# Hybrid attention block on one core: other durations and priorities in attention's list scheduler

## Chip, cores and metric

One core of a Trainium2 chip runs the whole kernel. The metric is the device time of one execution in microseconds (us). Three executions of the kernel before took 3311.18, 3316.16 and 3320.15 us; their median, 3316.16 us, is the time that the change is held against.

## What is computed

One transformer layer over 2048 tokens and 16 meta tokens, width 1024, in fp32: RMSNorm and one input projection, two groups of attention heads side by side, an output projection with a residual, then RMSNorm and a SwiGLU feed-forward part with a residual. Cut to the two attention groups:

```python
# group A: 8 query heads, 2 key heads, head width 64
p = jax.nn.softmax(sc, axis=-1).astype(va.dtype)
o = jnp.einsum('bkgql,blkd->bqkgd', p, va)
# group B: 4 heads; queries and keys in two halves j, values 128 wide
sc = jnp.einsum('bqhjd,blhjd->bhjql', q, kb).astype(jnp.float32) * scale
p = jax.nn.softmax(sc, axis=-1)
w = (p[:, :, 0] - lam * p[:, :, 1]).astype(vb.dtype)
o = jnp.einsum('bhql,blhe->bqhe', w, vb)
```

## The kernel before, in words

The kernel has three parts that follow each other: the input projection, attention, and output projection with the feed-forward part. Attention stands in an order that the kernel works out itself before anything runs; the other two parts are untouched.

Fp32 accuracy is had from fp16: a value is split into a high half (a cast) and a low half (value minus high half), and products are summed from the halves.

**Group B** has 64 *steps*, one for 128 queries of one head. Line numbers are those of the kernel before; in the changed kernel they are one higher from line 53 on. For each of its two score halves a step runs: score matmuls into a PSUM buffer `sy` (`score`, L482, PE); the *drain* of that buffer into SBUF with a running minimum (`minimum`, L489, DVE, 128x1024 a time, four a step); a bias (`peak`, L522, DVE); the exponential with its sum (`expo`, L517, ACT). Then two factors (L528, L532, DVE), the *difference* of the two halves (`diff`, L536, DVE, in two pieces), the cast to fp16 (`fp16_hi`, L112 with output `p`, ACT or DVE), the low half of that (`fp16_lo`, L549, five pieces, mostly POOL), a transposing DMA (`turn`, L585, on SP's queue) and 50 products with V (`pv`, L594, PE).

**Group A** has 32 *groups* of 128 queries and four heads. First a *reach*: plain scores into `sy` (`reach`, L498, PE) and their minimum over the keys (`lowest`, L502, DVE, eight of 128x1024 a group), a *merge* of these (L979, DVE), a flip of the merged column into a row (L985, PE) and the row itself (L992, DVE or ACT). Then nine *chunks* of turned scores: matmuls into `sy` (L512, L513, PE), exponential (`expo_a`, L555, ACT), high half (`hi_a`, L112 with output `hl`, ACT or DVE), *low half* (`lo_a`, L561, POOL or DVE), products with V (`pv_a`, L570, PE).

So three buffers `sy` are shared by everything that PE scores, and are freed by DVE (drain, reach, row) or ACT (chunks). One group and two steps make a *round*: from one merge L979 to the next. There are 32 merges.

The **list scheduler** (the loop at the end of attention) holds a list of tasks per engine. A task has a time from which it may start, an estimated cost, the buffers that it needs and an age. At each turn the engine that can start something earliest takes, of the tasks that can start then, the one with the lowest age, emits its instructions and frees itself after the estimated cost. `wait` and `later` add, for one engine of those that may take a task, a delay and an age. Tasks marked with `port` (low halves, differences, casts on DVE) are planned so that DVE and POOL never run one at the same time. The estimates only shape the order: on the chip each engine runs its instructions in that order, and semaphores do the rest.

```python
at = [(max([z["ready"] + z["wait"].get(n, 0.0), idle[n], port[0] if n in z["port"] else 0.0] + [when(k) for k in z["need"]]), z["age"] + z["later"].get(n, 0.0), i)
      for i, z in enumerate(todo[n])]
```

## Time and profile before

| | before |
|---|---|
| median of 3 runs (lowest, highest) | 3316.16 us (3311.18, 3320.15) |
| the profiled execution | 3310.24 us |
| its span, first to last instruction | 3308.4 us |
| mean granted TensorE clock | 0.99 |
| busy share of the span: PE, DVE, ACT, POOL | 95%, 62%, 50%, 50% |

The busy shares are averages over three parts with different limits. The page's chain that ended last gives PE 72%, DVE 11%, ACT 6%, time in which an engine waited for nothing that the profile shows 5%, DMA 4%. The largest lines of that chain, L1379 with 27% and L1340 with 14%, belong to the feed-forward part; those of attention (L594, L570, L482, L489, L555, L502, L536) have 2 to 4% each.

A row of the timeline gives start, duration, engine, line, operation, output<-input and count; a count over 1 means that neighbours of the same kind were merged. In brackets stands the idle time of the engine before it and what ended it.

### The profile page before, as it was taken

The numbers are of one execution on the slowest core, as the hardware profiler recorded it, in microseconds if no ns is written. First come the engines' busy times: TensorE is split into PE (matmuls) and PEld (weight loads), VectorE is DVE, ScalarE is ACT, GpSimd is POOL, SyncE is SP. The second block draws the span as 40 slices with busy tenths as digits, with TensorE's granted clock in tenths as the row PEclk, the third lists the DMA queues.
The fourth block names the chain that finished last, engine by engine and source line by source line (L and its number), as shares of the span: only waits on it lengthen the run. The fifth ranks groups of instructions, "written<-read, shape, count | busy, mean of one in ns | idle before, by whom it ended". The sixth has DMA issues, their size and how long they took to land.

```text
span 3308.4 us, 57942 instructions
## 1 busy us (share of the span) xinstructions
PE 3145.7 (95%) x23043; PEld 2069.5 (63%) x23043; DVE 2056.2 (62%) x3656; ACT 1639.2 (50%) x1991; POOL 1639.3 (50%) x1597
## 2 busy tenths in 40 slices
PE   8999988989988898888889999999999999999999
PEld 7999975655555565555568755555555555555555
DVE  7555568888888889888865334444444544444445
ACT  6333328888887888888866222222222322222220
POOL 6888866767676677676721133232232323232231
PEclk9999999999999999999999999999999999999999
DMA  5322233343243334433467511111111511111111
GB/s 168 72 68 68 67 85 74 78 109 88 73 111 81 84 86 100 88 83 74 107 236 259 165 58 55 42 58 42 54 52 45 174 50 51 45 58 39 57 45 51
DMA packets 503359, 281.35 MB, mean 85 GB/s; under 512 B 330704, under 2 KB 478624, under 8 KB 502576
## 3 DMA queue, kind: packets, MB, share of 16 engines
q1 hardware_dynamic: 501376, 275.14, 30.6%
q8 instruction: 181, 2.97, 0.4%
q10 hardware_dynamic: 1712, 2.51, 0.3%
q14 instruction: 90, 0.74, 0.1%
HBM read 168.44 MB, written 39.93 MB: 63 GB/s over the span
## 4 chain that ended last, share of the span: by engine, by line
PE 72%; DVE 11%; ACT 6%; issue 5%; DMA 4%; POOL 1%; SPq 0%; DVEq 0%; ACTq 0%; POOLq 0%
PE pg L1379 27%; PE psd L1340 14%; PE pl L269 10%; PE sy L482 4%; PE ob L594 4%; PE oa L570 3%; DVE e L489 3%; ACT et L555 2%; DVE mna L502 2%; PE ps L1285 2%; PE sy L498 2%; PE sy L512 2%; PE sy L513 2%; DVE e L536 2%; DMA wq<-in_w_up_dram 1%
## 5 line engine op out<-in xcount | busy, mean ns | idle before, releaser
L1342 DVE TENSOR_TENSOR y<-psd,y 128x512 f32<-128x512 f32 x704 | 484.8, 691 | 551.0 <-PE psd L1340 549.8
L561 POOL TENSOR_TENSOR hl<-et,hl 128x1024 f16<-128x1024 f32 (+1 forms) x247 | 520.9, 2128 | 303.8 <-ACT hl L112 168.7
L1379 PE MATMUL pg<-h2h,e 128*128 128x512 f16 x2112 | 660.0, 380 | 1.6 <-POOL e L116 1.6
L1379 PEld LDWEIGHTS <-e 128*128 128x128 f16 x3168 | 283.2, 98 | 390.3 <-issue 84.9
L1379 PE MATMUL pg<-h2l,e 128*128 128x512 f16 x1056 | 400.7, 380 | 0.0
L489 DVE CUSTOM_DVE_ANT_0 e<-sy,zero,mn 128x1024 f32<-128x1024 f32 x256 | 325.5, 1277 | 43.0 <-PE sy L482 37.8
L116 POOL TENSOR_TENSOR e<-qa,e 128x1024 f16<-128x1024 f32 (+1 forms) x44 | 100.0, 2273 | 498.8 <-issue 381.8
L555 ACT ACTIVATE et<-sy,lnpa,ndq 128x1024 f32<-128x1024 f32 (+1 forms) x288 | 322.1, 1145 | 39.6 <-PE sy L513 16.9
L549 POOL TENSOR_TENSOR p<-e,p 128x516 f16<-128x516 f32 (+2 forms) x320 | 311.4, 1006 | 50.7 <-ACT p L112 49.6
L1381 ACT ACTIVATE th<-pg,unh 128x512 f32<-128x512 f32 x88 | 60.5, 688 | 532.3 <-PE pg L1379 525.4
L1340 PE MATMUL psd<-kt,kt 128*128 128x512 f32 x1056 | 323.0, 434 | 0.0
L502 DVE TENSOR_REDUCE mna<-sy 128x1 f32<-128x1024 f32 x256 | 311.3, 1217 | 16.1 <-PE sy L498 15.5
L1340 PE MATMUL psd<-e,e 128*128 128x512 f32 x1056 | 320.5, 432 | 0.7 <-DVE y L1342 0.7
L517 ACT ACTIVATE e<-e,bs,ndq 128x2064 f32<-128x2064 f32 x128 | 269.2, 2103 | 92.2 <-DVE bs L522 92.2
L482 PE MATMUL sy<-kt,qb 128*128 128x512 f16 (+1 forms) x1280 | 284.3, 342 | 30.5 <-DVE mn L489 9.9
L570 PEld LDWEIGHTS <-hl 128*128 128x128 f16 (+1 forms) x6528 | 241.6, 97 | 91.3 <-issue 20.5
L570 PE MATMUL oa<-va,hl 128*128 128x65 f16 (+3 forms) x6528 | 261.8, 193 | 21.0 <-DVE hl L561 7.9
L112 ACT CAST hl<-et 128x1024 f16<-128x1024 f32 (+1 forms) x288 | 275.8, 991 | 6.8 <-PE oa L570 5.3
L116 POOL TENSOR_TENSOR kt<-qb,kt 128x1024 fp32r<-128x1024 f32 x22 | 52.7, 2397 | 442.8 <-issue 384.2
L594 PEld LDWEIGHTS <-pt 128*128 128x128 f16 (+2 forms) x3200 | 202.2, 98 | 72.9 <-issue 7.8
L1340 PEld LDWEIGHTS psd<-e,e 128*128 128x128 f32 x1056 | 198.8, 189 | 59.0 <-DVE y L1342 1.2
L1340 PEld LDWEIGHTS psd<-kt,kt 128*128 128x128 f32 x1056 | 199.0, 189 | 58.5
(229 smaller groups left out, 5775.4 us busy)
## 6 DMA issues: line engine op xcount, KB each, us to landing
wq<-in_w_gate_dram SPq DMA_DIRECT2D x16, 704.0 KB, 4.9
wq<-in_w_up_dram SPq DMA_DIRECT2D x16, 704.0 KB, 5.4
qa<-in_w_gate_dram SPq DMA_DIRECT2D x22, 512.0 KB, 3.9
qa<-in_w_down_dram SPq DMA_DIRECT2D x22, 512.0 KB, 3.7
qa<-in_w_up_dram SPq DMA_DIRECT2D x22, 512.0 KB, 3.8
qb<-in_w_up_dram SPq DMA_DIRECT2D x22, 512.0 KB, 3.7
qb<-in_w_down_dram SPq DMA_DIRECT2D x22, 512.0 KB, 3.6
qb<-in_w_gate_dram SPq DMA_DIRECT2D x22, 512.0 KB, 3.8
```

The lines of the kernel that those rows point to most:

```text
L269: T.matmul(ps[:rows, c0:UW], hb[:, a, k, :rows], w_at(w, ui, k)[:, c0:], start=(k == 0 and a == 0 and w == 0), stop=(k == KD - 1 and a == 1))
L482: T.matmul(y[:, (c - c0) // 512 if g_ else j, :n], qt[:, j, a, qi * P:(qi + 1) * P], kt[:, c:c + n], start=(a == 0), stop=(a == 1))
L489: V.tensor_tensor_reduce(e[:, c0:c1], src[:, :c1 - c0], zero.broadcast_to([P, c1 - c0]), 1.0, mn[:, g_ - 1:g_] if g_ else big, ALU.add, AL ...
L502: V.tensor_reduce(g["mn"][:, h, g_:g_ + 1], y.rearrange("p b n -> p (b n)"), axis=AX.X, op=ALU.min)
L549: eng.tensor_tensor(out=p[:, at + c0:at + c1], in0=st["e"][0][:, c0:c1], in1=p[:, c0:c1], op=ALU.subtract)
L555: A.activation(of(et, k), of(y, k), AF.Exp, bias=lnpa if k else lnpa[:NM], scale=ndq[:, 0:1] if k else ndq[:NM, 0:1])
L561: eng.tensor_tensor(out=of(z[:, 1], k), in0=of(et, k), in1=of(z[:, 0], k), op=ALU.subtract)
L570: T.matmul(o[:, h, :wn], z[:rows, a, i, h * P:(h + 1) * P], vt[:rows, c, vh, :wn], start=(first and h == 0 and n == 0), stop=(last and n = ...
L594: T.matmul(o, pt[:rows, blk, :], vt[:rows, c, vh, :], start=(c == 0 and n == 0), stop=(c == NC - 1 and n == 1))
L1340: T.matmul(ps, a[:, i * P:(i + 1) * P], w[:, 0, ns], start=(ii == 0), stop=(ii == 2))
L1342: V.tensor_tensor(out=yt[:, ns], in0=ps, in1=yt[:, ns], op=ALU.add)
L1379: T.matmul(ps, a[:, k], b_[:, k], start=(k == 0 and ii == 0), stop=(k == KD - 1 and ii == 2))
```

## The change

Only constants of the scheduler change, and six estimates.

- Estimated durations: the drain L489 1.22 to 1.36 us (`CM`); the reach keeps 1.22 under a name of its own (`CR`); the bias 0.07 to 0.12; the exponential of group B 2.0 to 2.29, of a chunk 1.08 to 1.19 (its small first chunk 0.6 to 0.75).
- Ages (lower goes first): turned scores `OPT` -2 to -1.5; drain and reach on DVE `OM` -2 to -1; group B's and the reach's scores on PE `OP` -2 to -1; bias, merge, flip and row `OB` -2 to 0; low half `OL` 3 to 0; products with V `OV` -10 to -10.5, which makes them later by 0.5.
- Which engine: DVE may take a chunk's low half without the 2 us delay that it had (`LWA` 2 to 0), at an age higher by 1 (`LLA` 0 to 1); DVE's high half of a chunk gets 6 instead of 3 (`HLA`).
- `HCUT` 2 to 1: a cast to fp16 that DVE took would be one piece, not two.

```diff
-HCUT = 2
+HCUT = 1
...
-CM = 1.22
+CM = 1.36
+CR = 1.22
...
-OPT = -2.0
-LWA, LLA, HWA, HLA = 2.0, 0.0, 50.0, 3.0
-OS, OX, OM, OD, OH, OP, OV, OE = -2.0, -1.0, -2.0, -2.0, 3.0, -2.0, -10.0, 2.0
+OPT = -1.5
+LWA, LLA, HWA, HLA = 0.0, 1.0, 50.0, 6.0
+OS, OX, OM, OD, OH, OP, OV, OE = -2.0, -1.0, -1.0, -2.0, 3.0, -1.0, -10.5, 2.0
...
-OB, OC, OL = -2.0, 0., 3.0
+OB, OC, OL = -2.0, 0., 0.0
...
-                            task(("act",), st["n"] + OX, end + X_, 2.0, x)
-                        task(("dve",), st["n"] + OB, end + 0.14, 0.07, bias)
+                            task(("act",), st["n"] + OX, end + X_, 2.29, x)
+                        task(("dve",), st["n"] + OB, end + 0.14, 0.12, bias)
...
-                task(("dve",), g["n"] - GS + h * GS / 4 + OM, end + 0.2, CM if g_ else 0.25, m)
+                task(("dve",), g["n"] - GS + h * GS / 4 + OM, end + 0.2, CR if g_ else 0.25, m)
...
-                task(("act",), age + OX, end + 0.2, 1.08 if k else 0.6, x, ("et",))
+                task(("act",), age + OX, end + 0.2, 1.19 if k else 0.75, x, ("et",))
```

What this makes of the order is seen at three places, all on DVE. In the rows `hl<-et` is a low half, `e<-e,rho,e` a difference, `e,mn<-sy` a drain, `mna<-sy` a reach, `qa<-sy` the row; numbers tell buffers apart.

The first place is the start of a late round, from the merge of the 27th group on. Before:

```order
L979 TENSOR_REDUCE mqa_19866<-mna_19476 128x4
L522 TENSOR_SCALAR bs_19883<-mn_19649,dq_102,lnpk_100 128x1
L561 TENSOR_TENSOR hl3_6614<-et3_6610,hl3_6614 128x1024
L992 TENSOR_SCALAR qa0_6581<-sy2_6619 1x512
L489 ISA e0_6585,mn_19942<-sy0_6617,zero_65,big_67 128x16
L489 ISA mn_19942 128x1
L489 ISA e2_6587,mn_19943<-sy0_6617,zero_65,big_67 128x16
L489 ISA mn_19943 128x1
L528 RECIPROCAL rc_19965<-sums_19647 128x2
L532 SCALAR_TENSOR_TENSOR rho_19967<-rc_19965,neglam_94,sums_19647 128x1
L536 SCALAR_TENSOR_TENSOR e4_6589<-e1_6586,rho_19967,e4_6589 128x1032 x2
L504 TENSOR_REDUCE mna_19988<-sy0_6617 128x4
```

and now:

```order
L980 TENSOR_REDUCE mqa_19851<-mna_19491 128x4
L607 TENSOR_SCALAR mix_19695<-ob0_6720,rc_19486 128x128
L523 TENSOR_SCALAR bs_19858<-mn_19663,dq_102,lnpk_100 128x1
L993 TENSOR_SCALAR qa0_6581<-sy0_6617 1x512
L537 SCALAR_TENSOR_TENSOR e4_6589<-e5_6590,rho_19744,e4_6589 128x1032 x2
L562 TENSOR_TENSOR hl5_6616<-et1_6608,hl5_6616 128x1024
L529 RECIPROCAL rc_19958<-sums_19661 128x2
L533 SCALAR_TENSOR_TENSOR rho_19972<-rc_19958,neglam_94,sums_19661 128x1
L490 ISA e2_6587,mn_19952<-sy2_6619,zero_65,big_67 128x16
L490 ISA mn_19952 128x1
L490 ISA e3_6588,mn_19953<-sy2_6619,zero_65,big_67 128x16
L490 ISA mn_19953 128x1
```

A whole difference that stood in the round before is now behind the row, and behind the rows shown the second difference follows; in this round DVE has three differences, in its neighbours one.

The second place is the middle of the same round, where the second step of the round begins. Before:

```order
L502 TENSOR_REDUCE mna_19988<-sy0_6617 128x1
L489 ISA e5_6590,mn_20188<-sy0_6617,zero_65,big_67 128x16
L489 ISA mn_20188 128x1
L489 ISA e3_6588,mn_20189<-sy0_6617,zero_65,big_67 128x16
L489 ISA mn_20189 128x1
L528 RECIPROCAL rc_20221<-sums_19941 128x2
L532 SCALAR_TENSOR_TENSOR rho_20226<-rc_20221,neglam_94,sums_19941 128x1
```

and now:

```order
L562 TENSOR_TENSOR hl2_6613<-et0_6607,hl2_6613 128x1024
L562 TENSOR_TENSOR hl3_6614<-et1_6608,hl3_6614 128x1024
L529 RECIPROCAL rc_20190<-sums_19951 128x2
L490 ISA e5_6590,mn_20127<-sy2_6619,zero_65,big_67 128x16
L490 ISA mn_20127 128x1
L490 ISA e0_6585,mn_20128<-sy2_6619,zero_65,big_67 128x16
L490 ISA mn_20128 128x1
L533 SCALAR_TENSOR_TENSOR rho_20203<-rc_20190,neglam_94,sums_19951 128x1
L537 SCALAR_TENSOR_TENSOR e2_6587<-e3_6588,rho_20203,e2_6587 128x1032 x2
```

Two low halves have come to DVE here, ahead of the factors.

The third place is the end of attention, around the last difference. Before:

```order
L561 TENSOR_TENSOR hl1_6612<-et3_6610,hl1_6612 128x1024
L561 TENSOR_TENSOR hl2_6613<-et0_6607,hl2_6613 128x1024
L606 TENSOR_SCALAR mix_22709<-ob0_6720,rc_22520 128x128
L528 RECIPROCAL rc_22938<-sums_22674 128x2
L532 SCALAR_TENSOR_TENSOR rho_22941<-rc_22938,neglam_94,sums_22674 128x1
L536 SCALAR_TENSOR_TENSOR e4_6589<-e1_6586,rho_22941,e4_6589 128x1032 x2
```

and now:

```order
L537 SCALAR_TENSOR_TENSOR e1_6586<-e2_6587,rho_22937,e1_6586 128x1032 x2
L562 TENSOR_TENSOR hl2_6613<-et0_6607,hl2_6613 128x1024
L562 TENSOR_TENSOR hl3_6614<-et1_6608,hl3_6614 128x1024
L550 TENSOR_TENSOR p16_1_6604<-e1_6586,p16_1_6604 128x516 x3
L550 TENSOR_TENSOR p16_1_6604<-e1_6586,p16_1_6604 128x500
L550 TENSOR_TENSOR p16_1_6604<-e1_6586,p16_1_6604 128x16
L562 TENSOR_TENSOR hl4_6615<-et2_6609,hl4_6615 128x1024
L562 TENSOR_TENSOR hl5_6616<-et3_6610,hl5_6616 128x1024
```

The low halves of the last step's `p` and of the last chunks, POOL's before, stand on DVE.

Counted over the program, no instruction is added or dropped but for where they run: DVE takes 70 of the 256 full low halves of chunks instead of 41, POOL 186 instead of 215; one small low half, the five pieces of one step's `p` and three small evacuations (L606 for L604) come to DVE as well. All 64 casts to fp16 are ACT's in both, so `HCUT` cuts nothing.

## Rows read from the trace of the kernel before

**Rows 1.** The page: span, and busy time of each engine.
```profile
span 3308.4 us, 57942 instructions
PE 3145.7 (95%) x23043; PEld 2069.5 (63%) x23043; DVE 2056.2 (62%) x3656; ACT 1639.2 (50%) x1991; POOL 1639.3 (50%) x1597
```

**Rows 2.** Timeline of DVE, the merge L979: first, last and nine between.
```profile
493.40 0.17 DVE L979 TENSOR_REDUCE mqa<-mna 128x4 f32<-128x12 f32 x1
...
695.55 0.16 DVE L979 TENSOR_REDUCE mqa<-mna 128x4 f32<-128x12 f32 x1
736.91 0.16 DVE L979 TENSOR_REDUCE mqa<-mna 128x4 f32<-128x12 f32 x1
...
842.39 0.16 DVE L979 TENSOR_REDUCE mqa<-mna 128x4 f32<-128x12 f32 x1
...
914.18 0.16 DVE L979 TENSOR_REDUCE mqa<-mna 128x4 f32<-128x12 f32 x1
...
987.84 0.15 DVE L979 TENSOR_REDUCE mqa<-mna 128x4 f32<-128x12 f32 x1
1034.68 0.16 DVE L979 TENSOR_REDUCE mqa<-mna 128x4 f32<-128x12 f32 x1
...
1282.15 0.16 DVE L979 TENSOR_REDUCE mqa<-mna 128x4 f32<-128x12 f32 x1
1323.74 0.16 DVE L979 TENSOR_REDUCE mqa<-mna 128x4 f32<-128x12 f32 x1
...
1470.53 0.16 DVE L979 TENSOR_REDUCE mqa<-mna 128x4 f32<-128x12 f32 x1
...
1619.55 0.15 DVE L979 TENSOR_REDUCE mqa<-mna 128x4 f32<-128x12 f32 x1
```

**Rows 3.** Windows, the shortest full round: stretch, length, busy of PE, PEld, DVE, ACT, POOL.
```profile
1249.09:1282.15 33.06, 31.75 (x402) 20.39 (x400) 30.86 (x56) 29.56 (x29) 21.52 (x17) 1.00 0.43 106
```

**Rows 4.** Timeline of DVE in the round from the merge at 1396.05.
```profile
1396.05 0.15 DVE L979 TENSOR_REDUCE mqa<-mna 128x4 f32<-128x12 f32 x1
...
1396.35 1.22 DVE L561 TENSOR_TENSOR hl<-et,hl 128x1024 f16<-128x1024 f32 x1
1397.48 0.67 DVE L992 TENSOR_SCALAR qa<-sy 1x512 f16<-1x512 f32 x1
...
1399.70 2.50 DVE L536 SCALAR_TENSOR_TENSOR e<-e,rho,e 128x1032 f32<-128x1032 f32 x2
1403.40 0.23 DVE L504 TENSOR_REDUCE mna<-sy 128x4 f32<-128x64 f32 x1 [1.20 <-PE sy L498]
...
1412.65 3.30 DVE L561 TENSOR_TENSOR hl<-et,hl 128x1024 f16<-128x1024 f32 x1
...
1421.08 4.37 DVE L536 SCALAR_TENSOR_TENSOR e<-e,rho,e 128x1032 f32<-128x1032 f32 x2
...
1426.51 1.27 DVE L489 CUSTOM_DVE_ANT_0 e<-sy,zero,mn 128x1024 f32<-128x1024 f32 x1
...
1427.71 1.21 DVE L502 TENSOR_REDUCE mna<-sy 128x1 f32<-128x1024 f32 x1
1428.85 1.27 DVE L489 CUSTOM_DVE_ANT_0 e<-sy,zero,mn 128x1024 f32<-128x1024 f32 x1
```

**Rows 5.** Timeline of POOL, the same round.
```profile
1409.53 8.41 POOL L561 TENSOR_TENSOR hl<-et,hl 128x1024 f16<-128x1024 f32 x4
```

**Rows 6.** Groups by line and form, 490 to 1660 us: busy, mean ns, idle before.
```profile
L561 POOL TENSOR_TENSOR hl<-et,hl 128x1024 f16<-128x1024 f32 x214 | 479.8, 2255 | 289.7 <-ACT hl L112 156.5 <-issue 116.8 <-DMA qa<-mix_scr 8.7
...
L561 DVE TENSOR_TENSOR hl<-et,hl 128x1024 f16<-128x1024 f32 x41 | 68.4, 1673 | 0.5 <-issue 0.5
```

**Rows 7.** Timeline of DVE, then of POOL, at the end of attention.
```profile
1638.30 7.85 DVE L561 TENSOR_TENSOR hl<-et,hl 128x1024 f16<-128x1024 f32 x1
...
1663.89 2.15 POOL L549 TENSOR_TENSOR p<-e,p 128x516 f16<-128x516 f32 x1
...
1667.12 4.92 POOL L549 TENSOR_TENSOR p<-e,p 128x516 f16<-128x516 f32 x4
```

## The prediction

> **What bounds the kernel now.** I read the page first: PE is busy 95% of the span and DVE 62% [rows 1]. That is an average; the change reorders only attention, so I looked there, with windows and with a clock made of the merge L979, one per round. The 32 merges run from 493.40 to 1619.55 us [rows 2]: 31 rounds in 1126.15 us, 36.33 us each. Three are long because a head's keys and values are exchanged in them: 41.36, 46.84 and 41.59 us, from 695.55, 987.84 and 1282.15 [rows 2], 129.79 together. The other 28 take 996.36, a mean of 35.58 us. They differ: the best has 33.06 us [rows 3], the two from 1396.05 on have 74.48 together [rows 2, 4], 37.24 each.
>
> The best round shows the floor: PE is busy 31.75, DVE 30.86, ACT 29.56 of 33.06 us [rows 3]. Three engines are nearly full, none can be relieved much, and a longer round is one in which they wait for each other. The late round shows how. DVE stands 1.20 us at L504 because PE could not score [rows 4]: all three `sy` buffers were held by turned scores that ACT had not drained. And DVE's low half takes 3.30 us instead of 1.22, the two pieces of a difference 4.37 instead of 2.50 [rows 4]: POOL was in the middle of four low halves of 2.1 us each [rows 5], and these operations do not run beside POOL's. The planner believes that it keeps the two apart; with wrong durations it doesn't. So 2.08 and 1.87 us are lost in one round.
>
> **The change, part by part.** *Work on each engine.* 29 full low halves go from POOL to DVE. The next row starts 1.13 us after one on DVE [rows 4]; on POOL one takes 2.10 [rows 5]. DVE gains 29 x 1.13 = 33 us, about one a round; POOL loses 61. The time in which DVE and POOL exclude each other falls by 29 x (2.10 - 1.13) = 28 us over attention. The moved small pieces are a few us. `HCUT` costs nothing and gains nothing, since no cast to fp16 is on DVE.
>
> *The order.* From about the sixth round on the new order repeats every two rounds, a light one with one difference and two low halves on DVE and a heavy one with three differences and three low halves. I price DVE's work in such a pair by the distance from one start to the next: 16 drains at 1.20 and 16 reaches at 1.14 (1426.51, 1427.71, 1428.85) [rows 4], 19.2 + 18.2; eight pieces of differences at 1.21 (2.50 for two that overlap by 0.08), 9.7; five low halves at 1.13, 5.7. For the small ones (row 0.67 [rows 4], biases, factors, evacuations, small drains) I take 4.1 us a round, an estimate: of the 30.86 us of the best round [rows 3], which has two low halves, the large ones are 9.6 + 9.1 + 4.8 + 2.3, which leaves 5.0, and I take off 0.9 for the ends of records that lie in waits. Together 61.0 us a pair.
>
> Then the waits. I walked one pair of the new order forward on paper, PE, DVE, ACT and POOL side by side, with these durations and three `sy` buffers. In the light round about 2.2 us of waiting are left: 0.5 for the second exponential before the factors, 0.6 at the first drain, 0.9 at the low half ahead of the second step, behind a POOL low half, and some tenths. In the heavy round 3.8: 0.8 around the row, which now has no low half ahead of it to fill the time of the flip; 1.0 in a difference that POOL's `p` pieces enter; 0.5 at the two low halves; 1.3 at reaches and drains late in the round. The stall at L504 is gone: differences and low halves, 7 us of work, fill the time in which ACT drains turned scores. That makes 67.0. A walk on paper misses collisions, so I add one more like that of the difference, 1.87 [rows 4]: **68.9 us a pair**, 34.45 a round. Ends for the pair: 66.1, twice the best round [rows 3], and 74.5, the late pair; I take the value near the first, since the walk accounts for each wait there.
>
> Of the 28 ordinary rounds 22 have the new pattern; the first five and one with a V conversion in it I leave at their mean, and the three exchanges too, whose waits for DMAs the change doesn't touch. Gain: 11 x (2 x 35.58 - 68.9) = 25 us.
>
> *The end of attention.* Before, DVE's low half at 1638.30 takes 7.85 us [rows 7], 6.6 more than one alone, because POOL runs a low half and five `p` pieces meanwhile; drains and chunks behind it wait. And the low half of the last `p` on POOL lasts from 1663.89 to 1672.04 [rows 7], 8.15 us, with everything after it waiting. Now DVE does that. No row has these pieces on DVE: half a piece of a difference, 0.6 us each, bounds it below, 2.6 in all; a POOL-like 4.9 above. Two low halves stand before it, 2.3. I take 4 us gained of 8.15 (ends 1 and 5.5), and half of the 6.6 us, 3.3, as another low half will meet POOL: **7 us**, ends 0 and 12.
>
> *What gives back.* DVE is 61 of 68.9 us full; what is late next is the row after the flip, and POOL's `p`: in the heavy round two steps' `p` run one after the other, and their transposes reach PE with some 1.5 us to spare in the walk.
>
> *Sum.* 3310.24 us, the profiled execution, - 25 - 7 = 3278. That execution lies 0.9 us under the lowest of the three timed runs and 5.9 under their median; I add 2 and predict **3280 us**, 1.1% under the median.
>
> **A rule against the change.** A low half that meets POOL on DVE takes 1.67 us in the mean, on POOL 2.26 [rows 6]. The Trainium skill (Perfetto Trace Analysis, Optimizing Scalar/DVE Operations) says that VectorE and GpSimd share an SBUF port, so that moving work between them may not help. By this rule the sum would keep DVE's 33 us and lose the 25. The rows give a mixed picture: collisions are there, yet the same work occupies both for 1.13 us on the one engine and 2.10 on the other, so the move shortens the shared time. It is the second rival below.
>
> **The durations.** The new 1.36 for a drain is its record, 1.27, and the 0.08 of the readout behind it; but the next instruction starts after 1.20 [rows 4]. So the plan believes DVE slower than it is, by 256 x 0.16 = 41 us over attention, and the old 1.22 was nearer as a distance. That a longer estimate orders better is no matter of course; the walk, not the estimate, carries my forecast. The Trainium skill (same page and section) says that a recorded latency covers time that overlaps the next instruction, as these rows do; by it the new constant would be wrong for throughput.
>
> **Rivals.** 0.3% of 3316, 10 us, is about what a measurement of this kernel can tell from no change.
> 1. *Forecast:* pairs of 67 to 70.5 us, 3260 to 3302. Chance 0.58.
> 2. *Nothing gained:* DVE's added 33 us lie on the path and the waits only move. For it: in the pair from 842.39 to 914.18, in which DVE has four low halves, 71.79 us pass [rows 2] although POOL hardly disturbs it. With 71.8 a pair: 11 x 0.64 = +7, - 4 at the end: 3313, with the 2 us 3315. Chance 0.15, of which 0.03 is faster by over 0.3%.
> 3. *Slower: POOL enters between the pieces.* In the heavy round three differences and three low halves must each find POOL idle. Where POOL's low half is ready between two of them, it takes 2.1 us and DVE waits 1.87 [rows 4]. In my walk the margin is under 1 us at three of these places. Three more such waits make 68.9 + 5.6 = 74.5, as the late pairs have: 11 x 3.34 = +37, and no gain at the end: 3347, with the 2 us 3349. Two more (72.6) are where it becomes slower than before. Against it: POOL has 61 us less work, and stands idle behind ACT's casts 156.5 us in all [rows 6]. Chance 0.15.
> 4. *More gained:* pairs at the floor of 66.1, the end at 12 us: 11 x 5.06 + 12 = 68, 3242, with the 2 us 3244. Chance 0.12.
>
> That the change doesn't do what it says can be excluded: the order shows it.
>
> **Numbers.** Faster by over 0.3%: 0.58 + 0.12 + 0.03 = 0.73; within: 0.12; slower: 0.15. The range goes from 3246, close to the floor, to 3330, which leaves out most of rival 3; about 0.08 is outside below and 0.12 above. The forecast's own range is 3260 to 3302.
>
> **What would show it.** The distance of merges in the late rounds: two in turn, near 31 and 38 us, together 67 to 70.5; by rival 2 near 72, by rival 3 near 74. No stall of 1 us at L505 in the heavy round. Differences with 2.50 us for two pieces; where 4.4 shows up in more than one place of a pair, rival 3 is at work. POOL's busy time in attention lower by 60 us, DVE's higher by about 30 less what collisions shrink. The last `p` on DVE in under 5 us, attention's end earlier by the sum. Wrong would be my pair if DVE waits for PE at transposed `p` (L595), which never held PE up before.

## The result and the profile after

The changed kernel takes **3264.04 us** (median of 4 runs, 3262.35 to 3266.65) against 3313.67 us of the kernel before in the same comparison (4 runs, 3310.13 to 3320.15): a ratio of 0.985, 95% interval 0.983 to 0.9867, so 49.6 us or 1.5% faster. The forecast was 3280 us, 36 us under the median of 3316.16 us that it was worked out against and 34 under this one. The profiled execution of the changed kernel took 3266.65 us with a span of 3264.9 us, 43.5 us under the span before [rows 1]; the working below is against the spans.

Line numbers are one higher than before, since a constant was added. First the page of the changed kernel.

```profile
span 3264.9 us, 57936 instructions
...
PE 3130.3 (96%) x23043; PEld 2065.4 (63%) x23043; DVE 2085.0 (64%) x3694; ACT 1651.0 (51%) x1988; POOL 1574.2 (48%) x1562
```

POOL has 65 us less to do, DVE 29 us more [rows 1]. That is the moved work, and it does not tell why 43 us are gone: POOL is busy half of the span in both, and DVE is now busier.

The groups by line and form in attention tell more, 490 to 1620 us of the changed kernel (busy, mean ns; then the idle time of the engine before them, and what ended it).

```profile
L562 POOL TENSOR_TENSOR hl<-et,hl 128x1024 f16<-128x1024 f32 x186 | 410.8, 2228 | 175.0 <-ACT hl L113 102.6 <-issue 47.3 <-PE sy L986 14.4
...
L518 ACT ACTIVATE e<-e,bs,ndq 128x2064 f32<-128x2064 f32 x128 | 269.4, 2105 | 15.7 <-DVE bs L523 14.2
...
L499 PE MATMUL sy<-kt,qa 128*128 128x512 f16 x496 | 150.3, 385 | 13.3 <-DVE mn L490 7.1 <-DVE mna L503 4.1 <-DVE mna L505 1.8
...
L562 DVE TENSOR_TENSOR hl<-et,hl 128x1024 f16<-128x1024 f32 x70 | 101.7, 1468 | 0.4 <-ACT hl L113 0.3
...
L505 DVE TENSOR_REDUCE mna<-sy 128x4 f32<-128x64 f32 x31 | 6.7, 218 | 0.1
```

The same view of the kernel before, 490 to 1660 us, for three of these lines:

```profile
L517 ACT ACTIVATE e<-e,bs,ndq 128x2064 f32<-128x2064 f32 x128 | 269.2, 2103 | 92.2 <-DVE bs L522 92.2
...
L498 PE MATMUL sy<-kt,qa 128*128 128x512 f16 x496 | 150.2, 385 | 41.8 <-DVE mna L502 33.1 <-DVE mn L489 4.6 <-ACT et L555 3.1
...
L504 DVE TENSOR_REDUCE mna<-sy 128x4 f32<-128x64 f32 x31 | 7.0, 225 | 32.6 <-PE sy L498 32.6
```

Read the last column. The work per instruction is the same, but the waits have shrunk: ACT waited 92.2 us ahead of group B's exponentials for the bias on DVE, now 15.7 in all and 14.2 for the bias; PE 41.8 us ahead of the reach's matmuls, now 13.3; DVE 32.6 us for the first scores of a round, now 0.1. That last one is the stall of 1.20 us of [rows 4], which came 26 times in the kernel before.

The steady rounds are an exact clock. Windows of the changed kernel for a light and a heavy round that follow one another (columns as in [rows 3], then TensorE's granted clock, DMA share and GB/s), and for comparison the late pair of the kernel before:

```profile
1442.57:1472.83 30.26, 29.64 (x363) 19.00 (x360) 28.31 (x51) 28.76 (x29) 19.48 (x14) 1.00 0.47 97
1472.83:1509.87 37.04, 33.89 (x451) 21.80 (x449) 35.09 (x58) 32.95 (x31) 27.17 (x21) 1.00 0.33 80
```

```profile
1396.05:1470.53 74.48, 64.82 (x810) 41.36 (x807) 65.53 (x105) 60.85 (x60) 51.84 (x35) 1.00 0.34 79
```

Together the new pair has 67.30 us, against 74.48 before [rows 2, 4]. DVE is busy 63.40 us of it and idle 3.9; before it was busy 65.53 and idle 9.0. Wherever the pair stands free in the 31 rounds it has this length within 0.15 us. The 31 rounds take 1085.4 us (1126.15 before [rows 2]).

| Part, us | before | forecast | measured |
|---|---|---|---|
| 22 rounds of the new pattern (at the mean before) | 782.9 | 758 | 734.2 |
| first five rounds (at the mean before) | 177.9 | 177.9 | 176.6 |
| round with a V conversion (at the mean before) | 35.6 | 35.6 | 39.9 |
| three exchange rounds | 129.8 | 129.8 | 134.7 |
| last merge to the end | 1688.9 | 1681.9 | 1687.7 |

With 1.6 us before the first merge these make the 43.5 us. Against the mean of before, the new pattern gave twice what was forecast, 48.6 us, and 9 us were lost again around the conversions of V (into two fp16 halves, L445 and L447). The mean hides something: by their own times in the kernel before, the first five rounds took 169.1 us, the round with a V conversion 36.1 and the other 22 rounds 791.2. So the new pattern gave 57.0 us against the rounds that it replaced, and the first five rounds lost 7.5.

### The profile page after: what moved, and what is told of

The parts are those of the page before. It is cut to its first block, busy times and chain, and to the rows that moved or that the text cites. A ratio compares the mean times of both kernels' runs of the same rounds, so it can differ in the third digit from the quotient of the medians.

```text
span 3264.9 us, 57936 instructions
## 1 busy us (share of the span) xinstructions
PE 3130.3 (96%) x23043; PEld 2065.4 (63%) x23043; DVE 2085.0 (64%) x3694; ACT 1651.0 (51%) x1988; POOL 1574.2 (48%) x1562
## 4 chain that ended last, share of the span: by engine, by line
PE 80%; DVE 10%; DMA 4%; issue 3%; ACT 2%; POOL 1%; SPq 0%; DVEq 0%; ACTq 0%; POOLq 0%
PE pg L1380 27%; PE psd L1341 14%; PE pl L270 11%; PE sy L483 5%; PE ob L595 5%; PE oa L571 5%; PE sy L513 3%; PE sy L514 3%; PE ps L1286 3%; DVE e L490 3%; DVE mna L503 2%; PE sy L499 2%; DVE e L537 2%; DMA wq<-in_w_gate_dram 1%; PE pt L130 1%
## 5 line engine op out<-in xcount | busy, mean ns | idle before, releaser
L562 POOL TENSOR_TENSOR hl<-et,hl 128x1024 f16<-128x1024 f32 (+1 forms) x217 | 447.7, 2082 | 244.5 <-ACT hl L113 154.4
L550 POOL TENSOR_TENSOR p<-e,p 128x516 f16<-128x516 f32 x315 | 324.1, 1062 | 106.9 <-ACT p L113 89.8
L518 ACT ACTIVATE e<-e,bs,ndq 128x2064 f32<-128x2064 f32 x128 | 269.4, 2105 | 15.7 <-DVE bs L523 14.2
L571 PEld LDWEIGHTS <-hl 128*128 128x128 f16 (+1 forms) x6528 | 229.0, 98 | 52.5 <-issue 15.9
L571 PE MATMUL oa<-va,hl 128*128 128x65 f16 (+3 forms) x6528 | 246.8, 194 | 6.5 <-POOL hl L562 2.3
L513 PE MATMUL sy<-qa,kt 128*128 128x512 f16 (+1 forms) x544 | 208.0, 382 | 33.9 <-DVE mna L503 27.9
L1341 PEld LDWEIGHTS psd<-kt,kt 128*128 128x128 f32 x1056 | 198.9, 189 | 58.9
```

Source lines behind the costliest of these rows:

```text
L550: eng.tensor_tensor(out=p[:, at + c0:at + c1], in0=st["e"][0][:, c0:c1], in1=p[:, c0:c1], op=ALU.subtract)
L562: eng.tensor_tensor(out=of(z[:, 1], k), in0=of(et, k), in1=of(z[:, 0], k), op=ALU.subtract)
L571: T.matmul(o[:, h, :wn], z[:rows, a, i, h * P:(h + 1) * P], vt[:rows, c, vh, :wn], start=(first and h == 0 and n == 0), stop=(last and n = ...
L1341: T.matmul(ps, a[:, i * P:(i + 1) * P], w[:, 0, ns], start=(ii == 0), stop=(ii == 2))
```

## Experiments

*Correction to the part on the change:* the diff leaves `OB` at -2; of that line only `OL` changes. No step of the prediction rests on it.

Two theories stood against mine (T: the time follows from where the order puts differences and low halves). R1: the gain is low halves moved from POOL to DVE. R2: it is durations nearer to the chip's. A *meeting*, below, is a DVE operation that takes longer because POOL is in one of its own.

**1. Durations alone.** The kernel before with the five changed estimates.

```diff
-CM = 1.22
+CM = 1.36
+CR = 1.22
...
-task(("act",), st["n"] + OX, end + X_, 2.0, x)
+task(("act",), st["n"] + OX, end + X_, 2.29, x)
```

> The kernel before with the changed durations alone (drain 1.36, reach 1.22, difference step 2.29, chunk 1.19 and 0.75, bias 0.12); its priorities stay. T (the time follows from whether the order puts the differences and low halves where ScalarE already drains scores, so that a light and a heavy round make 67.3 us): the order that comes out has 22 full low halves on VectorE and no light and heavy rounds by turns, much like that of the kernel before, so 3300 to 3320 us. R1 (the gain is low halves moved from GpSimd to VectorE): fewer of them than before, so 3314 or more. R2 (the gain comes from durations that are nearer to the chip's): 3275 or less.

Measured: 3322.81 us, ratio 1.0029 (1.0019 to 1.0038). R2 falls: the durations alone make the kernel a little slower. T's range ended 3 us lower; R1, which asked for 3314 or more, holds here too.

**2. Priorities alone.** The changed kernel with the old estimates.

> The changed kernel with the old durations, so the changed priorities alone. Its order has 55 full low halves on VectorE (the changed kernel 70); the late rounds come in pairs of a light and a heavy one as in the changed kernel, the early ones are irregular. T: 3270 to 3290 us, late pairs of rounds at 67 to 69 us, early ones longer. R1 (work moved to VectorE): about half of the gain, near 3285. R2 (durations): no gain, 3310 to 3318.

Measured: 3299.97 us, ratio 0.9962 (0.9947 to 0.9977). 13 of the 49.6 us. All three missed the total: 10 us over T's range. T's part on the late rounds holds: from the 24th round on they are 30.0 and 38.7 us by turns, 68.6 a pair, but the irregular rounds from the 9th to the 14th take 248.5 us, against 218.0 for the same ones before and 211.5 in the changed kernel. These 37 us are the whole of its lag behind the changed kernel. Neither half of the change gives the gain by itself; it needs an order that settles into the pattern early.

**3. One line of priorities: more low halves on DVE.**

```diff
-LWA, LLA, HWA, HLA = 2.0, 0.0, 50.0, 3.0
+LWA, LLA, HWA, HLA = 0.0, 1.0, 50.0, 3.0
```

> The kernel before with one line of the priorities changed, the low halves' (0, 1 in place of 2, 0): 96 of them on VectorE, more than in the changed kernel (70). T: the order has no light and heavy rounds by turns and puts low halves behind the differences, so no gain in proportion: 3305 to 3335 us. R1: the more on VectorE the faster, below 3264. R2: no gain, near 3314.

Measured: 3358.07 us, ratio 1.0138 (1.0122 to 1.0154). The kernel with most work moved to DVE is 44.8 us slower than before, 23 more than T allowed. POOL's busy time is 1519.2 us on its page, the least of the kernels that compute everything. R1 falls.

**4. Places undone, amount of work kept.**

```diff
-OS, OX, OM, OD, OH, OP, OV, OE = -2.0, -1.0, -1.0, -2.0, 3.0, -1.0, -10.5, 2.0
+OS, OX, OM, OD, OH, OP, OV, OE = -2.0, -1.0, -2.0, -2.0, 3.0, -2.0, -10.0, 2.0
```

> The changed kernel with the offsets of the merge (OM), of the reach and P (OP) and of V (OV) put back to -2, -2 and -10. 68 low halves on VectorE, as many as in the changed kernel, durations the changed ones, but the rounds are irregular. T: 3285 to 3310 us, since the place of the steps and not their number makes the gain. R1 and R2: no difference from the changed kernel, 3260 to 3270.

Measured: 3327.05 us, ratio 1.0042 (1.0026 to 1.0058): 63 us slower than the changed kernel with nearly the same work on each engine (DVE 2104.7 us, POOL 1574.9, on its page). So the gain needs these three offsets, taken together, and R1 and R2, which asked for 3260 to 3270, fall; the loss is again larger than I expected. (`OM` is the offset of drains and reaches on DVE, not of the merge, as the expectation calls it.)

**5. The low halves' priorities undone.** The changed kernel with `LWA, LLA` at 2, 0. It still has 64 full low halves on DVE, 6 fewer.

> The changed kernel with the low halves' priorities put back (2, 0 in place of 0, 1). Its order has the same light and heavy rounds from the sixth round on and 64 low halves on VectorE in place of 70; only the first rounds and the tail are ordered differently. T (the light and heavy rounds make the gain): pairs of 67.3 us again, 3258 to 3276 us. R1 (the low halves moved to VectorE make it): 6 of 29 given back, some 8 to 10 us slower, near 3273; and if the low halves' own priority is what sets the place of the steps, 3300 or more.

Measured: 3265.79 us, ratio 0.9856 (0.9829 to 0.9883), no different from the changed kernel. Pairs are 67.3 us. This part of the change, the one that reads as if it moved the work, adds nothing here, and alone it loses (experiment 3). With `HCUT` it is the same, without a run: put back to 2 it gives the same program, instruction for instruction.

**6 and 7. POOL's low halves cut short,** in the order before and in the changed one. The first chunk's small low halves stay whole; of the others POOL subtracts 8 of 512 columns per half and leaves the rest out. (Both runs also clear the low halves' buffers once, ahead of attention; those lines are left out here.)

```diff
+            if eng is G and k:
+                eng.tensor_tensor(out=z[:, 1, :, :8], in0=et[:, :, :8], in1=z[:, 0, :, :8], op=ALU.subtract)
+                return
             eng.tensor_tensor(out=of(z[:, 1], k), in0=of(et, k), in1=of(z[:, 0], k), op=ALU.subtract)
```

> The kernel before in its own order, where GpSimd's low half of a chunk subtracts 8 of its 512 columns per half and leaves the rest out, so that GpSimd is soon done and seldom meets VectorE's pieces. The merge-to-merge rounds held 58 us of such meetings in all. T (the waits are the order's own, meetings are the smaller part): 25 to 50 us faster than the kernel before, 3265 to 3290. Rival C (what the change removes is meetings with GpSimd's runs, and nothing else): 50 us or more, at or below 3264.

> The same shortened low halves on GpSimd in the changed kernel's order. Its rounds held 52 us of meetings. T: its light and heavy pair has little waiting left, but the exchange rounds lose their 7 us waits, so 15 to 40 us faster than the changed kernel, 3225 to 3250, and still 30 us or more ahead of the shortened kernel before. Rival C: within 15 us of the shortened kernel before.

Measured: 3254.05 us (ratio 0.9823, 0.9801 to 0.9845) and 3221.71 us (0.9729, 0.9706 to 0.9752). The kernel before gains 56 us, 6 more than T's range allowed (11 us under its 3265) and as much as C asked. But the shortened changed kernel is still 32.3 us ahead of the shortened kernel before, as T asked and C excludes; it gains 42 us itself, just above T's range. So of the 49.6 us some 32 stay when POOL's long low halves are gone and belong to the order on PE, DVE and ACT; the other 17 are meetings with POOL, and lateness of POOL's low halves, which cost less in the new order. The shortening removes both at once and cannot part them. By rounds the shares differ: the 22 rounds of the new pattern are 57.0 us shorter than those that they replaced, and 24.7 with the short low halves, so in them POOL has more than half of the gain. The kernel as a whole shows less of that, because the changed order has more meetings elsewhere: they lengthen DVE's operations by 14 us in the first five rounds (1 before) and by 31 in the four rounds with a conversion of V (20 before).

Where meetings cost is seen by setting two timelines side by side. DVE in the light round of the changed kernel from 1375.27, with two lines of the heavy round:

```profile
1375.27 0.16 DVE L980 TENSOR_REDUCE mqa<-mna 128x4 f32<-128x12 f32 x1
...
1378.85 0.17 DVE L529 RECIPROCAL rc<-sums 128x2 f32<-128x2 f32 x1 [0.70 <-ACT e L518]
...
1392.69 1.87 DVE L562 TENSOR_TENSOR hl<-et,hl 128x1024 f16<-128x1024 f32 x1
...
1405.54 0.16 DVE L980 TENSOR_REDUCE mqa<-mna 128x4 f32<-128x12 f32 x1
...
1412.00 3.40 DVE L537 SCALAR_TENSOR_TENSOR e<-e,rho,e 128x1032 f32<-128x1032 f32 x2
...
1425.72 3.17 DVE L562 TENSOR_TENSOR hl<-et,hl 128x1024 f16<-128x1024 f32 x2
...
1442.57 0.16 DVE L980 TENSOR_REDUCE mqa<-mna 128x4 f32<-128x12 f32 x1
```

The same pair with POOL's low halves short:

```profile
1332.89 0.16 DVE L985 TENSOR_REDUCE mqa<-mna 128x4 f32<-128x12 f32 x1
...
1350.31 1.22 DVE L567 TENSOR_TENSOR hl<-et,hl 128x1024 f16<-128x1024 f32 x1
...
1363.15 0.16 DVE L985 TENSOR_REDUCE mqa<-mna 128x4 f32<-128x12 f32 x1
...
1369.62 3.40 DVE L539 SCALAR_TENSOR_TENSOR e<-e,rho,e 128x1032 f32<-128x1032 f32 x2
...
1383.33 2.35 DVE L567 TENSOR_TENSOR hl<-et,hl 128x1024 f16<-128x1024 f32 x2
...
1400.19 0.16 DVE L985 TENSOR_REDUCE mqa<-mna 128x4 f32<-128x12 f32 x1
```

The low halves' meetings (1.87 for 1.22, 3.17 for 2.35) are gone, and the pair is 67.30 us long again. In the new pattern these 1.5 us lie beside other waits and cost nothing. In the order before they cost: the last six rounds take 223.5 us whole and 206.4 us shortened, the changed kernel 201.9 us both ways, so 17.1 of the 21.6 us gained there go with POOL's low halves. And one wait stands in the order before even with the short low halves, the stall at the first scores. Timeline of DVE, the shortened kernel before:

```profile
1436.84 0.23 DVE L506 TENSOR_REDUCE mna<-sy 128x4 f32<-128x64 f32 x1 [1.20 <-PE sy L500]
...
1438.18 1.28 DVE L491 CUSTOM_DVE_ANT_0 e<-sy,zero,mn 128x1024 f32<-128x1024 f32 x1 [1.11 <-PE sy L484]
```

**8. A faster version: V conversions kept off POOL's runs.** Experiment 7 shortened the exchange rounds from 46.3 and 46.7 us to 37.0, the length of a heavy round. Their trace in the changed kernel shows why; DVE, then POOL, in the exchange round from 1261.13:

```profile
1281.36 7.23 DVE L447 SCALAR_TENSOR_TENSOR vb<-e,vsc,vb 128x2048 f16<-128x2048 f32 x1
1288.51 2.20 DVE L447 SCALAR_TENSOR_TENSOR vb<-vx,vsc,vb 32x128 f16<-32x128 f32 x1
1290.82 1.89 DVE L533 SCALAR_TENSOR_TENSOR rho<-rc,neglam,sums 128x1 f32<-128x1 f32 x1
```

```profile
1279.02 7.42 POOL L562 TENSOR_TENSOR hl<-et,hl 16x512 f16<-16x512 f32 x4
1287.02 5.67 POOL L562 TENSOR_TENSOR hl<-et,hl 128x1024 f16<-128x1024 f32 x2 [0.58 <-POOL hl L562]
```

V's low half waits until POOL's four low halves are through, and ACT then waits 6.94 us for the difference behind it. The planner did not know that this step uses what POOL uses:

```diff
-                    task(("dve",), age, end + X_, 2.4 if unit[0] == "b" else 1.3, lo_)
+                    task(("dve",), age, end + X_, 2.4 if unit[0] == "b" else 1.3, lo_, port=BOTH)
```

> The changed kernel, with the planner told that VectorE's low half of a V unit uses both engines' port (as it is told for differences and low halves), so that it is not put beside a run of GpSimd's low halves. The light and heavy rounds stay; the exchange rounds have GpSimd's run elsewhere. T: exchange rounds of 38 to 42 us in place of 46 and 47, so 10 to 20 us faster than the changed kernel, 3244 to 3255. If those rounds are long for another reason (PE's extra turned scores and V units), within 4 us of the changed kernel.

Measured: **3251.38 us** (3247.3 to 3253.86), ratio 0.9814 (0.9791 to 0.9837). That is 12.7 us under the changed kernel, and no run of the one reaches into the runs of the other. The two stood in different comparisons; against the kernel before in each, the gains are 58.9 and 49.6 us, which is 9.3 apart. It is the fastest kernel here that computes everything. Groups of this kernel in attention:

```profile
L447 DVE SCALAR_TENSOR_TENSOR vb<-e,vsc,vb 128x2048 f16<-128x2048 f32 x4 | 10.9, 2737 | 0.0
```

Four conversions take 10.9 us where they took 19.6 (4894 ns each). The exchange rounds are 42.5, 39.8 and 43.7 us instead of 46.3, 41.7 and 46.7: a third of the way only, two of them above what T asked, because now a difference in them meets POOL's low halves (5.31 us for two pieces that take 2.50). Of the span's 16.3 us the exchange rounds gave 8.7, the round with a V conversion 4.7 (35.2 us instead of 39.9), the first five rounds, which came out in another order, 4.1, and the part before the first merge 1.5; after the last merge 3.1 were lost.

**9. Durations from start to start.** The changed kernel with drain 1.20, reach 1.14, group B's exponential 2.10 (the "difference step" of the expectation; ACT's, not DVE's), chunk 1.09 and 0.57, bias 0.19.

> The changed kernel with durations set to the measured distances from one start to the next (drain 1.20, reach 1.14, difference step 2.10, chunk 1.09 and 0.57, bias 0.19) in place of the recorded lengths. The priorities stay. Its order has 51 low halves on VectorE and no repeating pair of rounds. T (a regular pattern with the pieces in the right places makes the gain, and no duration is better for being truer): 3280 to 3300 us. Rival R2 (durations nearer to what an engine's queue really advances by give the better order): 3264 or less.

Measured: 3299.93 us, ratio 0.9968 (0.9956 to 0.998). As T has it, and R2 falls again. The prediction called the new 1.36 for a drain too long by 0.16; as a distance it is, and yet the plan made with 1.20 and the other nearer durations is 36 us slower.

**10. The drain at 1.33 in place of 1.36,** in the kernel of experiment 8.

> The kernel whose V low halves are marked as using both engines' port (the version that took 3251 us), with the drain's duration at 1.33 in place of 1.36. That constant alone brings another order: from the fifth round on every round is alike, with two differences and one low half on VectorE, 57 low halves in all. T (what counts is that differences and low halves lie where ScalarE drains turned scores; taking turns of light and heavy rounds is only one way to that): rounds of 33 to 34 us, near the pair's mean of 33.65, and 3235 to 3262 us. Rival A (the light and heavy turns themselves are what fits, as in the changed kernel): rounds of 35 us or more, 3270 or above. R1 (more low halves on VectorE): slower than 3251 by about 13 x 1.1 = 14 us.

Measured: 3374.17 us, ratio 1.019 (1.0173 to 1.0207). Nothing expected this: 123 us for 0.03 us in an estimate. (Of full low halves 51 are on DVE, not 57.) A's number is met, its reason is not the one in the trace. The order is nearly as regular as said: 17 of the 31 rounds have the same instructions in the same order on each engine, and 14 of these take 41.1 to 41.2 us. DVE from one low half to the next:

```profile
1288.20 4.01 DVE L562 TENSOR_TENSOR hl<-et,hl 128x1024 f16<-128x1024 f32 x1
...
1294.34 1.85 DVE L533 SCALAR_TENSOR_TENSOR rho<-rc,neglam,sums 128x1 f32<-128x1 f32 x1
1296.22 4.33 DVE L537 SCALAR_TENSOR_TENSOR e<-e,rho,e 128x1032 f32<-128x1032 f32 x2
...
1313.80 4.37 DVE L537 SCALAR_TENSOR_TENSOR e<-e,rho,e 128x1032 f32<-128x1032 f32 x2
...
1329.36 3.99 DVE L562 TENSOR_TENSOR hl<-et,hl 128x1024 f16<-128x1024 f32 x1
```

and POOL at these places:

```profile
1283.69 7.43 POOL L562 TENSOR_TENSOR hl<-et,hl 16x512 f16<-16x512 f32 x4
1294.03 4.22 POOL L562 TENSOR_TENSOR hl<-et,hl 128x1024 f16<-128x1024 f32 x2 [2.92 <-ACT hl L113]
...
1314.38 2.70 POOL L562 TENSOR_TENSOR hl<-et,hl 128x1024 f16<-128x1024 f32 x1 [5.03 <-issue]
...
1324.83 7.43 POOL L562 TENSOR_TENSOR hl<-et,hl 16x512 f16<-16x512 f32 x4
```

From 1288.20 to 1329.36 it is 41.16 us. Over their length alone the four meetings cost 2.79 (4.01 for 1.22), 1.63 (1.85 for 0.22), 1.83 and 1.87 (for 2.50): 8.12 us, and without them the round would be 33.0 if nothing else changed. The plan believes these steps apart; on the chip they meet, and because every round is alike they meet in every round. That is rival 3 of the prediction, in an order that lies 0.03 us beside the one that was forecast.

One of the 17 rounds shows what the meetings are worth. In it DVE waits 1.43 us for PE and so comes past POOL:

```profile
1546.67 0.16 DVE L980 TENSOR_REDUCE mqa<-mna 128x4 f32<-128x12 f32 x1
...
1558.06 0.18 DVE L576 RECIPROCAL rA<-oa 128x4 f32<-128x4 f32 x1 [1.43 <-PE oa L571]
...
1566.96 1.22 DVE L562 TENSOR_TENSOR hl<-et,hl 128x1024 f16<-128x1024 f32 x1
...
1571.17 0.21 DVE L533 SCALAR_TENSOR_TENSOR rho<-rc,neglam,sums 128x1 f32<-128x1 f32 x1
1571.41 2.50 DVE L537 SCALAR_TENSOR_TENSOR e<-e,rho,e 128x1032 f32<-128x1032 f32 x2
```

Windows of a stretch before the end of that wait, of this round, and of another of the 17 (columns as before):

```profile
1555.00:1558.00 3.00, 3.00 (x30) 1.90 (x28) 1.63 (x3) 3.00 (x4) 1.82 (x2) 0.50 0.00 0
1546.67:1582.82 36.15, 33.07 (x402) 21.23 (x402) 31.06 (x52) 30.83 (x30) 25.30 (x18) 0.95 0.34 82
834.26:873.90 39.64, 31.77 (x402) 20.51 (x402) 37.03 (x52) 30.74 (x30) 27.36 (x19) 1.00 0.34 74
```

PE's granted clock is 0.50 in that stretch, the lower of its two levels (1.2 GHz), after PE had waited 0.77 and 1.28 us in the 3 us before it fell. Three of the four meetings are gone, 6.2 us of lengthening, and the same instructions take 36.15 us, 5.0 less. The round from 834.26 has all four meetings but a granted clock of 1.00, where the rounds of 41.1 us have 0.96; it takes 39.64, so about 1.5 us of the 41.1 go with the clock.

**11. Meant to shorten POOL's low halves in that order.**

> The kernel of the regular rounds (drain's duration 1.33, V low halves marked), in its own order, with GpSimd's low half of a chunk cut to 8 of its 512 columns per half; the rest is left out. In each of its 41.1 us rounds the profile showed four VectorE operations that met GpSimd's runs: a low half of 4.0 us, a factor of 1.9, two differences of 4.3, together 8 us more than alone. T (these meetings, which this order repeats in every round, are the whole of its loss): rounds of 33 to 35 us and 3190 to 3240 us, 130 us or more faster than uncut. Rival O (the order itself, its place of differences and drains, is bad): rounds of 37 us or more, above 3280.

Measured: 3252.76 us, ratio 0.9822 (0.9807 to 0.9837). The kernel that ran was not the one described: it was the shortened kernel before once more (41 low halves on DVE, rounds as in experiment 6), and it repeats that run's 3254.05 us. It says nothing on its question. That meetings are the whole loss of experiment 10 is not shown. The round from 1546.67 shows that three of the four are worth 5.0 us of the round.

**12. The drain at 1.42.**

> The kernel with marked V low halves and the drain's duration at 1.42. Again another order: pairs of rounds with two differences each, one round with four low halves on VectorE and one with one, 66 low halves in all. It is an attempt at a faster version. If the meetings are few, as in the changed kernel: pairs of 67 to 69 us, 3245 to 3265 us. If its rounds repeat meetings as those of the drain at 1.33 do: pairs of 72 us or more, above 3290. The order alone does not tell which.

Measured: 3313.56 us, ratio 1.0003 (0.9993 to 1.0013), no gain. (59 full low halves are on DVE, not 66.) The time is that of the second case; the late pairs are 71.7 us, between the two cases that I had set. Meetings don't explain them: in the groups by form its differences take 1471 ns, its factors 222 and its V conversions 2418, no more than in the changed kernel; only the low halves take more, 1583. This order is slower by its own waits, as windows of a late pair show (columns as before):

```profile
1553.86:1625.61 71.75, 64.67 (x804) 41.44 (x804) 63.16 (x105) 61.15 (x59) 48.68 (x35) 1.00 0.34 82
```

DVE is busy 63.16 us, as in the changed kernel's pair (63.40), and idle 8.6 us instead of 3.9.

## Why the prediction was right, and where it was off

- **The bound.** It named three nearly full engines that wait for each other, and one stall that shows it [rows 3, 4]. Right: the gain is waiting removed, 92.2 to 15.7 us at ACT's exponential and 32.6 to 0.1 at DVE's first scores, while the work on DVE grew. In the late pair DVE's idle time fell from 9.0 to 3.9 us. Experiments 3 and 4 show that as much work or more on DVE in other places loses. (One reading was loose: the difference of 4.37 us in [rows 4] did not meet the four low halves of [rows 5], which had ended at 1417.94, but two later ones, from 1421.99 on.)
- **The pair of rounds.** The walk on paper gave 67.0 us (61.0 of DVE's work and 6.0 of waits), the chip 67.30. Without the 2.4 us that meetings added, DVE was busy 61.0 us of it, as priced. The larger waits are there one by one: 0.5 us forecast for the second exponential and 0.70 measured, 0.9 for the low half behind POOL's and 0.65 measured (1.87 for 1.22), 1.0 for the difference that `p` pieces enter and 0.9 measured (3.40 for 2.50), 0.5 for two low halves and 0.8 measured. (Those listed for the heavy round add up to 3.6 us, not to the 3.8 that the sum used.)
- **The step that failed in size: "so I add one more like that of the difference, 1.87".** No further meeting came, and those that came cost nothing in this pattern: experiment 7 removes 1.5 us of meetings from the pair and leaves it at 67.30. Without this addition the sum would have been 11 x (71.16 - 67.0) = 46 us for the pattern, against 48.6 measured. Of these, 6 us are a matter of which rounds: the 22 hold twelve light ones and ten heavy ones, since the three exchange rounds stand where heavy ones would and the round with a V conversion where a light one would.
- **"... and the three exchanges too, whose waits for DMAs the change doesn't touch."** Wrong: 134.7 us against 129.8, and 39.9 for the round with a V conversion. In none of these exchange rounds, before or after, does a wait of PE, DVE or ACT end with a DMA. With POOL's low halves short they take 107.8 us in all; V's low half meets POOL's run in either order (3938 ns in the mean before, 4894 now). The clock has a part in it that no run separates: the granted clock of the three is 0.93, 0.92 and 0.89 in the changed kernel, 0.96, 0.89 and 0.92 before, and 1.00 in each with the short low halves. In the last of them in the changed kernel it is 0.50 from 1288.7 to 1298.9; PE stands idle from 1286.1 to 1293.1 there, for a drain behind V's low half. The first five rounds, left at the mean as well, are 7.5 us longer than their own time before.
- **The end of attention, 7 us.** The events came as forecast, even larger, and hardly reached the end. The last `p` is on DVE at the lower bound that the prediction had set (2.6), and the low half that took 7.85 us [rows 7] takes 1.98. Timeline of DVE, changed kernel:

```profile
1604.11 1.98 DVE L562 TENSOR_TENSOR hl<-et,hl 128x1024 f16<-128x1024 f32 x1 [0.26 <-ACT hl L113]
...
1611.41 2.58 DVE L550 TENSOR_TENSOR p<-e,p 128x516 f16<-128x516 f32 x5
```

  The first evacuated tile of the output projection then comes 65.4 us after the last merge instead of 78.5. But the eight tiles from there take longer. Windows of that stretch, first the changed kernel, then the kernel before (columns as in [rows 3], the last two DMA share and GB/s):

```profile
1642.60:1742.70 100.10, 93.04 (x443) 74.61 (x443) 54.16 (x93) 69.50 (x113) 11.23 (x14) 0.98 0.81 279
```

```profile
1698.10:1788.30 90.20, 85.72 (x418) 68.95 (x417) 53.52 (x91) 64.86 (x106) 12.81 (x14) 1.00 0.82 294
```

  Ten of the 13 us are given back there, and 1.2 us are left at the end. DMA is busy four fifths of either stretch, and ACT waits 30.5 us for the gate and up weights between the projection's first matmul and the feed-forward, 23.2 before. The projection seems to have run into the stream of weights; that no run tested.
- **The durations.** "A longer estimate orders better is no matter of course; the walk, not the estimate, carries my forecast." Experiments 1, 2 and 9 bear this out: new durations alone lose, truer ones lose, and the walk of the order that came out held to 0.3 us.
- **Rivals.** Rival 2, DVE's work on the path, gave 71.8 us a pair; experiment 12 has nearly that, but in its own order. Rival 3 decides from two more meetings a pair: in the forecast order there was none, at 1.33 us there are four a round. Rival 4's pair of 66.1 us was not reached, and of its 12 us at the end of attention 1.2 were left.
- **The rule on moving work** between engines that exclude each other would have kept DVE's added 33 us and given nothing. Measured: 1.5% gained, though the moved work without its places loses (experiments 3 and 4).

## What to carry to other kernels

With a list scheduler on three nearly full engines, judge the order that comes out and not the constants that made it: walk one repeating stretch by distances from start to start, with every wait, and count which operations can meet. A pattern that repeats repeats its meetings too, so measure each candidate: 0.03 us in one estimate cost 123 us here. Tell the planner of every step that uses a shared resource; one forgotten mark on a step that runs six times came with 9 to 13 us.

## What the runs showed of the hardware that I had not expected

A DVE operation that reads two operands from SBUF can wait through several POOL instructions, not just the one that is running: 7.23 us for V's low half, whose mean is 2346 ns where POOL's low halves are short (experiment 7). It began in the second of four low halves that POOL ran in 7.42 us without a gap, and came through only after the fourth. Elsewhere the two took turns: two pieces of a difference and two low halves of POOL, 5.31 and 5.21 us (experiment 8). The Trainium skill (SBUF — State Buffer, SBUF: two separate sides) says that of a DVE operation with two SBUF inputs and a GpSimd operation that reads SBUF, whichever starts first holds the shared pair of ports for its whole instruction and the other blocks; the rows agree on the blocking, and show that at the seam between two POOL instructions DVE need not come in. Tiny operations pay the same price: a factor of 128x1 elements takes 0.22 us alone and 1.85 behind a low half of POOL.

In experiment 10 a stretch at half of TensorE's clock made a round 5.0 us shorter: the wait for PE moved DVE past three meetings.

The kernel with POOL's low halves cut short in the order before also shows how much such meetings can cost: the excess of DVE's low halves, differences, factors and V conversions over their length alone falls from 71 us to 7, and the time by 56 us. (Means by form, before and cut: 41 low halves of 1673 and 1234 ns, 128 pieces of 1501 and 1296, 64 factors of 439 and 218, 4 conversions of 3938 and 2341; alone I take 1220, 1250, 218 and 2341.)
